# Computing the projection of a gated table in pieces between other products, with the results kept in DRAM

## The chip, the cores and the metric

One Trainium2 chip; the kernel runs on one of its cores. The metric is the device time of one execution in microseconds (us), median of the runs. All tensors are float32; a product of two float32 matrices is made of three matmuls of split operands (high x high, high x low, low x high), so every operand that enters TensorE is first split into a high part H (a cast on ScalarE) and a low part L = operand - H (a subtract on VectorE).

## The reference

One layer of a bidirectional hybrid encoder, 1024 positions, width 2048:

```python
z = rms_norm(h, norm_mix) @ w_in            # q, k, v, gate_a, u, gate_s
y_attn = block_attention(q, k, v) * silu(gate_a)
y_ssm = gelu(s5_bidirectional(u, ...))
glu = y_ssm @ w_glu + b_glu
y_ssm = glu[..., :1024] * sigmoid(glu[..., 1024:]) * silu(gate_s)
h = h + concatenate([y_attn, y_ssm]) @ w_out
gate = sigmoid(rms_norm(h, norm_ple) @ w_ple_gate)
h = h + gate * (p @ w_ple_proj)             # p: 1024 x 256
out = rms_norm(h, norm_final)
```

The change concerns the last product but one, `p @ w_ple_proj` (256 x 2048): it needs nothing that the layer computes, only inputs.

## The kernel before

Everything is transposed: a tile holds 128 features by positions. The work runs in stages whose instructions are written out by hand in one order for all engines (a manual schedule; each engine runs its own instructions in that order and waits on semaphores). In turn: the input projection with the state-space part beside it, attention (64 query blocks, `attention`, then four last iterations b = 64 to 67 that only finish blocks; 64 is NB), three stages of *units* in `back`, and the *gate*.

**Units.** Stages 0 (w_glu), 1 and 2 (halves of w_out) have 8 units each. A unit (`unit`) is a Strassen-like scheme of 7 products; a product is 4 x 3 = 12 matmuls of 512 columns into one PSUM tile `pr` (tag C, four buffers). Its weights are loaded by `sw_dma` (four 256 KB blocks a unit) and split by `sw_prep` three products ahead (two ScalarE copies, one VectorE subtract, L451, with a PSUM tile `hp` between). The result goes to the unit's thread (`u_glu`, `u_out`), which reads it on VectorE or ScalarE. All units of a stage share 28 split activation tiles `st` (4 per product). Those of the next stage are loaded (`put`) and split (`fill`, L311, in stage 2 L314) during the last unit, u = 7, into buffers that the products of that unit give back.

**Background work.** `bg` registers a generator; each `tick` advances all of them by one step and lets one waiting `fill` go out (four of five times in the units). There is a tick after each group of three matmuls of a unit's product and after every second group in the gate.

**Gate.** Two halves of 512 positions, in each 16 tiles n (`gate`): `mm_half` makes pg, 16 k-steps x 3 matmuls over w_gate, and then pp, 2 x 3 matmuls over w_proj, with the split halves of p that `p_load` makes at the start of each half. `fin_g` takes both: pg times the row scale, a sigmoid, times pp (L1352), plus h (on GpSimd, L1354). Weight blocks of 512 columns come through `w_dma` (three raw buffers) and `w_split`, in the order planned by `w_plan`, where each tile has four blocks of w_gate and one half-size block of w_proj. All DMAs are issued by SyncE's queue (SP), in program order.

## Time and profile before

| | |
|---|---|
| median of 3 runs | 2137.52 us (2135.57 to 2140.13) |
| profiled execution | 2138.92 us |
| its span, first to last instruction | 2137.1 us |
| mean granted TensorE clock | 0.989 of full speed |

A line such as L1185 is a line of the kernel before. PE is TensorE, PEld its weight loads, DVE VectorE, ACT ScalarE, POOL GpSimd, SP SyncE. In the windows PEclk is the clock granted to TensorE as a share of full speed, and "(x112)" a count of instructions. On a timeline a bracket gives the idle time of that engine before the instruction and what ended it. Matmuls are pipelined: the duration beside one is its latency, and the distance of two starts is what it costs.

### The profile page before, as it was taken

To read this page: it belongs to the slowest core of one execution; us is meant where nothing else is said; L and a number is where in the kernel's file an instruction comes from. 1 tells how busy PE (TensorE), PEld (TensorE's weight loads), DVE (VectorE), ACT (ScalarE), POOL (GpSimd) and SP (SyncE) were. 2 spreads that over 40 slices of the span, in tenths; PEclk is the share of its full clock that TensorE was granted. 3 is DMA by queue.
4 is the path that set the end of the run, shared out by engine and by line. 5 is a ranking of instruction groups with operands and counts; after the bars stand their busy time and mean duration, and the time that the engine had idled before them with its cause. 6 is when DMAs were issued, how large, how long until landed. Compare 5 with 4: busy or idle time off the path is not lost.

```text
span 2137.1 us, 29682 instructions
## 1 busy us (share of the span) xinstructions
PE 2064.0 (97%) x10140; PEld 1716.5 (80%) x10140; DVE 1475.1 (69%) x2406; ACT 901.2 (42%) x1615; POOL 922.8 (43%) x833
## 2 busy tenths in 40 slices
PE   8999999999999999998999999989999999999996
PEld 6888878888887877787889878878878778888885
DVE  7654787788877787847998976764677744465434
ACT  7111322122222222347777765654565633353332
POOL 0143455554655555513320556467565611221122
PEclk9999999999999999999999999999999999999998
DMA  6333223233333233454421366658765544455443
GB/s 217 91 107 104 78 72 113 83 84 95 94 85 109 79 88 94 143 173 148 158 70 50 129 236 213 227 194 285 252 200 168 173 143 125 134 183 168 148 117 123
DMA packets 183127, 296.51 MB, mean 139 GB/s; under 512 B 28352, under 2 KB 78656, under 8 KB 182720
## 3 DMA queue, kind: packets, MB, share of 16 engines
q1 hardware_dynamic: 181824, 292.51, 43.1%
q8 instruction: 81, 1.33, 0.3%
q10 hardware_dynamic: 1152, 2.10, 0.3%
q14 instruction: 70, 0.57, 0.1%
HBM read 211.37 MB, written 77.92 MB: 135 GB/s over the span
## 4 chain that ended last, share of the span: by engine, by line
PE 48%; DVE 8%; DMA 3%; ACT 2%; issue 2%; SPq 0%; POOL 0%; DVEq 0%; ACTq 0%
PE pr L1185 6%; PE pr L1186 6%; PE pr L1187 6%; PE pg L1325 5%; PE pg L1324 5%; PE pg L1326 5%; PE ptr L1017 2%; PE zgs L579 1%; PE zgs L580 1%; PE zgs L582 1%; PE S L987 1%; PE S L986 1%; PE S L990 1%; PE pv L1030 1%; PE pv L1031 1%
## 5 line engine op out<-in xcount | busy, mean ns | idle before, releaser
L311 DVE TENSOR_TENSOR wL<-wraw,wH 128x512 fp32r<-128x512 f32 x304 | 260.3, 870 | 317.0 <-ACT wH L310 312.9
L310 ACT CAST wH<-wraw 128x512 fp32r<-128x512 f32 x304 | 176.5, 595 | 302.2 <-PE zu L580 73.8
L1185 PE MATMUL pr<-st,wH 128*128 128x512 f32 x672 | 263.9, 393 | 11.9 <-DVE cx L1275 7.1
L1187 PE MATMUL pr<-st,wL 128*128 128x512 f32 x672 | 264.0, 393 | 0.4 <-DVE wL L451 0.4
L1186 PE MATMUL pr<-st,wH 128*128 128x512 f32 x672 | 263.6, 392 | 0.2 <-DVE st L311 0.2
L1326 PE MATMUL pg<-st,wL 128*128 128x512 f32 x512 | 200.1, 391 | 4.3 <-DVE wL L311 4.3
L1324 PE MATMUL pg<-st,wH 128*128 128x512 f32 x512 | 200.9, 392 | 0.7 <-ACT st L313 0.3
L1325 PE MATMUL pg<-st,wH 128*128 128x512 f32 x512 | 200.5, 392 | 0.6 <-DVE st L314 0.6
L1354 POOL TENSOR_TENSOR h<-cx,tz 128x512 f32<-128x512 f32 x31 | 40.8, 1318 | 295.0 <-DVE tz L1352 160.7
L1185 PEld LDWEIGHTS pr<-st,wH 128*128 128x128 f32 x672 | 127.3, 189 | 41.3 <-ACT st L310 5.9
L899 ACT COPY ks<-kp 16x224 f32<-16x224 f32 x32 | 10.8, 336 | 336.1 <-DVE ks L898 207.9
L1187 PEld LDWEIGHTS pr<-st,wL 128*128 128x128 f32 x672 | 127.3, 189 | 28.4 <-DVE wL L451 2.1
L1186 PEld LDWEIGHTS pr<-st,wH 128*128 128x128 f32 x672 | 127.2, 189 | 27.0 <-DVE st L311 0.6
L1326 PEld LDWEIGHTS pg<-st,wL 128*128 128x128 f32 x512 | 96.5, 189 | 25.3 <-DVE wL L311 5.1
L1324 PEld LDWEIGHTS pg<-st,wH 128*128 128x128 f32 x512 | 96.5, 188 | 23.1 <-ACT xsq L1342 1.0
L449 ACT CAST wH<-sraw 128x512 fp32r<-128x512 f32 x120 | 74.3, 619 | 96.7 <-PE pr L1186 75.9
L1267 POOL TENSOR_TENSOR cx<-cx,tz 128x512 f32<-128x512 f32 x64 | 87.8, 1384 | 62.6 <-DVE tz L1299 41.4
L1325 PEld LDWEIGHTS pg<-st,wH 128*128 128x128 f32 x512 | 96.4, 188 | 21.9 <-DVE st L314 1.3
L451 DVE TENSOR_TENSOR wL<-sraw,hp 128x512 fp32r<-128x512 f32 x120 | 81.9, 683 | 43.0 <-ACT hp L450 35.8
L772 POOL TENSOR_TENSOR tab<-pa 128x512 f32<-128x512 f32 x32 | 41.4, 1293 | 152.0 <-DVE r L907 152.0
L579 PE MATMUL zga<-hH,wH 128*128 128x512 f32 x256 | 104.6, 409 | 0.0
L579 PE MATMUL zq<-hH,wH 128*128 128x512 f32 x256 | 103.6, 405 | 0.0
(377 smaller groups left out, 5558.5 us busy)
## 6 DMA issues: line engine op xcount, KB each, us to landing
wraw<-in_w_in_dram SPq DMA_DIRECT2D x144, 256.0 KB
wraw<-in_w_gate_dram SPq DMA_DIRECT2D x128, 256.0 KB
sraw<-in_w_out_dram SPq DMA_DIRECT2D x64, 256.0 KB
st<-d_t SPq DMA_DIRECT2D x48, 256.0 KB
sraw<-in_w_glu_dram SPq DMA_DIRECT2D x32, 256.0 KB
cx<-in_xT_dram SPq DMA_DIRECT2D x16, 512.0 KB
d_p<-cx SPq DMA_DIRECT2D x16, 512.0 KB
cx<-d_p SPq DMA_DIRECT2D x16, 512.0 KB
```

The source lines that it names most:

```text
L310: nc.scalar.copy(H, src)
L311: nc.vector.tensor_tensor(L, src, H.bitcast(F32), ALU.subtract)
L449: self.nc.scalar.copy(H, raw)
L451: self.nc.vector.tensor_tensor(L, raw, hp, ALU.subtract)
L579: nc.tensor.matmul(ps[h], H[:, kk, :], rH[:, s], start=(k == 0), stop=False)
L1185: nc.tensor.matmul(ps, H[:, k], x[0], start=(k == 0), stop=False)
L1186: nc.tensor.matmul(ps, H[:, k], x[1], start=False, stop=False)
L1187: nc.tensor.matmul(ps, L[:, k], x[0], start=False, stop=(k == 3))
L1267: nc.gpsimd.tensor_tensor(x[:, h], x[:, h], u, ALU.add)
L1324: nc.tensor.matmul(ps, H[:, k % 4], x[0], start=(k == 0), stop=False)
L1325: nc.tensor.matmul(ps, H[:, k % 4], x[1], start=False, stop=False)
L1326: nc.tensor.matmul(ps, L[:, k % 4], x[0], start=False, stop=(k == nk - 1))
```

## The change

31 of the 32 projection products are made before or at the start of the gate, each as one *filler* (`filler`): 6 matmuls into a half of a PSUM tile `pp_ps`. Where they stand is listed in `F_AT` (stage, unit, product): four in the first unit of stage 0, four each in the last unit of stages 0, 1 and 2 and in the first of stages 1 and 2. Besides these there are four in the last four iterations of attention and three inside gate tile 0 (k = 1, 5, 9). The splits of p lie in the tiles "zz" and "t4" (`f_table`), made anew in unit 6 of each stage. Weights come in one raw tile `fR` and one split pair `fH`, `fL`; the results leave PSUM through one tile `po` and are stored in DRAM (`d_pp`). The gate loads them beside d_h into one tile (`x[:, 0]`, `x[:, 1]`); only its last tile still makes its product there. Further, the weight ring `sraw` has 5 buffers for 6, two small tiles `Bm` move to the pool of the state-space part, and the `hp` tiles take the halves of one PSUM tile for two tiles in turn.

```diff
@@ -249,2 +249,8 @@
 
+    F_AT = (
+        {(0, 0, i) for i in (1, 2, 4, 5)}
+        | {(s, 7, i) for s in range(3) for i in (3, 4, 5, 6)}
+        | {(s, 0, i) for s in range(1, 3) for i in (0, 1, 2, 4)}
+    )
+
     def __init__(self, ctx, tc, ins, out):
@@ -375,6 +381,7 @@
         self.w_end = len(q)
-        for _ in range(2):
+        for hf in range(2):
             for n in range(16):
                 tile_(self.i["w_gate"][n], 16)
-                tile_(self.i["w_proj"][n], 2)
+                if (hf, n) == (1, 15):
+                    tile_(self.i["w_proj"][n], 2)
         self.wq = q
@@ -427,3 +434,3 @@
             for j in blocks:
-                r = self.bk.tile([128, 512], F32, name="sraw", tag="sraw", bufs=6)
+                r = self.bk.tile([128, 512], F32, name="sraw", tag="sraw", bufs=5)
                 self.nc.sync.dma_start(r, self.su[u][j])
@@ -447,3 +454,3 @@
         raw = self.sr[src].rearrange("p (k m) -> p k m", m=128)
-        hp = self.ps.tile([128, 4, 128], F32, name="hp", tag="A", bufs=2)
+        hp = self.hp_ps[:, self.half(g % 2)].rearrange("p (k m) -> p k m", m=128)
         self.nc.scalar.copy(H, raw)
@@ -497,7 +504,2 @@
         self.rope_t = c.tile([128, 2, 64], F32, name="rope_t")
-        self.Bm = []
-        for j in range(2):
-            t = c.tile([128, 2, 2, 48], F32, name=f"Bm{j}")
-            nc.gpsimd.memset(t, 0.0)
-            self.Bm.append(t)
         self.rq = c.tile([128, NH * T], F32, name="rq")
@@ -525,2 +527,3 @@
         self.d_t = [[d(f"d_t{s}_{k}", (2, 128, SEQ)) for k in range(4)] for s in range(3)]
+        self.d_pp = [d(f"d_pp{n}") for n in range(KD)]
         self.d_pa = d("d_pa", (128, NG, NPA))
@@ -1173,3 +1176,3 @@
 
-    def unit(self, X, thread, nxt, hook):
+    def unit(self, s, u, X, thread, nxt, hook):
 
@@ -1192,2 +1195,4 @@
             hook(i)
+            if (s, u, i) in self.F_AT:
+                self.filler()
 
@@ -1313,2 +1318,63 @@
 
+
+    def f_table(self, hf):
+
+        self.fx = None
+        x = [self.t2k(tag, (128, 2, 512), F32R) for tag in ("zz", "t4")]
+        for k in range(2):
+            raw = self.bk.tile([128, 512], F32, name="po", tag="po", bufs=1)
+            self.nc.sync.dma_start(raw, self.i["pT"][k][:, self.half(hf)])
+            for _ in range(4):
+                yield
+            self.split(x[k][:, 0], x[k][:, 1], raw)
+            raw = None
+            yield
+        self.fx = x
+
+    def f_dma(self):
+        if self.fn < 31:
+            self.fraw = self.bk.tile([128, 256], F32, name="fR", tag="fR", bufs=1)
+            self.nc.sync.dma_start(self.fraw, self.i["w_proj"][self.fn % 16])
+            self.fn += 1
+
+    def f_split(self):
+        if self.fi < 31:
+            H, L = (self.bk.tile([128, 2, 128], F32R, name=t, tag=t, bufs=1) for t in ("fH", "fL"))
+            self.split(H, L, self.fraw.rearrange("p (k m) -> p k m", m=128))
+            self.fw, self.fraw = (H, L), None
+
+    def f_start(self):
+        self.f_dma()
+        for _ in range(5):
+            yield
+        self.f_split()
+        yield
+        self.f_dma()
+
+    def f_end(self, n, ps):
+        yield
+        o = self.bk.tile([128, 512], F32, name="po", tag="po", bufs=1)
+        self.nc.scalar.copy(o, ps)
+        self.f_split()
+        yield
+        self.f_dma()
+        yield
+        self.nc.sync.dma_start(self.d_pp[n % 16][:, self.half(n // 16)], o)
+
+    def filler(self):
+        n = self.fi
+        (H, L), self.fw = self.fw, None
+        ps = self.pp_ps[:, self.half(n % 2)]
+        for k in range(2):
+            x = self.fx[k]
+            self.nc.tensor.matmul(ps, H[:, k], x[:, 0], start=(k == 0), stop=False)
+            self.nc.tensor.matmul(ps, H[:, k], x[:, 1], start=False, stop=False)
+            self.nc.tensor.matmul(ps, L[:, k], x[:, 0], start=False, stop=(k == 1))
+            if k == 0:
+                self.tick()
+        self.fi += 1
+        del H, L
+        self.bg(self.f_end(n, ps))
+        self.tick()
+
     def mm_half(self, ps, nk, xs, each=None):
@@ -1411,3 +1477,3 @@
         for k in range(2):
-            H, L = (self.bk.tile([128, 512], F32R, name="sraw", tag="sraw", bufs=6) for _ in range(2))
+            H, L = (self.bk.tile([128, 512], F32R, name="sraw", tag="sraw", bufs=5) for _ in range(2))
             self.split(H, L, raw[k])
@@ -1424,4 +1490,5 @@
         hs, pT = [], {}
-        acc = self.t2k(("zz", "t4")[hf])
-        self.bg(self.p_load(hf, pT))
+        if hf == 1:
+            acc = self.t2k("t4")
+            self.bg(self.p_load(hf, pT))
         for n in range(16):
@@ -1430,4 +1497,7 @@
             pg = self.psC("pg")
-            ho = self.bk.tile([128, 512], F32, name="cx", tag="cx", bufs=4)
-            nc.sync.dma_start(ho, self.d_h[n][:, sl])
+            last = (hf, n) == (1, 15)
+            x = self.bk.tile([128, 2, 512], F32, name="cx", tag="cx", bufs=4)
+            nc.sync.dma_start(x[:, 0], self.d_h[n][:, sl])
+            if not last and (hf, n) != (0, 0):
+                nc.sync.dma_start(x[:, 1], self.d_pp[n][:, sl])
             if hf == 0 and n == 0:
@@ -1438,8 +1508,15 @@
                 self.mm_half(pg, 16, hg, lambda k: k < 15 and self.put_h(nhg, 1, [9 + k // 2], wait=3))
+            elif (hf, n) == (0, 0):
+                self.mm_half(pg, 16, hg, lambda k: self.fi < 31 and k % 4 == 1 and self.filler())
+                nc.sync.dma_start(x[:, 1], self.d_pp[n][:, sl])
+                self.fx = None
+                acc = self.t2k("zz")
             else:
                 self.mm_half(pg, 16, hg)
-            pp = self.psC("pp")
-            self.mm_half(pp, 2, pT)
+            pp = x[:, 1]
+            if last:
+                pp = self.psC("pp")
+                self.mm_half(pp, 2, pT)
             hs.append(hp[:, n % 2])
-            self.bg(self.fin_g(hf, n, pg, pp, ho, hs[n], acc))
+            self.bg(self.fin_g(hf, n, pg, pp, x[:, 0], hs[n], acc))
         if hf == 1:
@@ -1490,3 +1567,7 @@
                 self.bg(self.t_make(s + 1, stages[s + 1][0], self.four_sm, 14, 8))
-            self.unit(X, thread, units[n + 1][2] if n + 1 < len(units) else None, hook)
+            if u == 6:
+                self.bg(self.f_table(min(s, 1)))
+            elif u == 1:
+                self.fx = None
+            self.unit(s, u, X, thread, units[n + 1][2] if n + 1 < len(units) else None, hook)
             if u == 7:
@@ -1499,2 +1580,3 @@
         self.gate(0, hg, nhg)
+        assert self.fi == 31
         self.gate(1, nhg, None)
@@ -1569,2 +1651,7 @@
                 self.sp = ssm_pool.__enter__()
+                self.Bm = []
+                for n in range(2):
+                    t = self.sp.tile([128, 2, 2, 48], F32, name=f"Bm{n}", tag=f"Bm{n}")
+                    self.nc.gpsimd.memset(t, 0.0)
+                    self.Bm.append(t)
                 self.ssm_gen = self.ssm()
@@ -1583,2 +1670,10 @@
         for b in attn:
+            if b == NB - 5:
+                self.fn = self.fi = 0
+                self.bg(self.f_start())
+            elif b >= NB:
+                if b == NB:
+                    self.pp_ps = self.psA("pp_ps")
+                    self.hp_ps = self.psA("hp_ps")
+                self.filler()
             if b == 3:
@@ -1592,2 +1687,3 @@
                 self.sw_dma(0, range(4))
+                self.bg(self.f_table(0))
             elif b == NB - 4 or b == NB - 2:
```

## Rows read from the trace of the kernel before

**Rows 1.** The page, busy time of each engine, share of the span, instructions.
```profile
PE 2064.0 (97%) x10140; PEld 1716.5 (80%) x10140; DVE 1475.1 (69%) x2406; ACT 901.2 (42%) x1615; POOL 922.8 (43%) x833
```

**Rows 2.** TensorE's timeline inside a unit, first and last of 97 matmuls in sequence.
```profile
1359.73 0.39 PE L1187 MATMUL pr<-st,wL 128*128 128x512 f32 x1
...
1381.49 0.39 PE L1187 MATMUL pr<-st,wL 128*128 128x512 f32 x1
```

**Rows 3.** Instructions of line L1324 on tile pp: durations min/median/max in ns.
```profile
L1324 PE MATMUL pp<-sraw,wH x64: 392/394/398, 1725.7 to 2113.9; 128*128 128x512 f32 x64
```

**Rows 4.** Windows: busy us of PE, PEld, DVE, ACT, POOL, PEclk, DMA share, GB/s.
```profile
1226.00:1250.00 24.00, 22.25 (x97) 16.89 (x97) 20.18 (x28) 17.84 (x31) 9.02 (x7) 1.00 0.69 242
1380.00:1410.00 30.00, 23.61 (x88) 17.93 (x87) 29.38 (x37) 16.62 (x30) 16.43 (x13) 0.89 0.65 229
1395.00:1400.00 5.00, 5.00 (x16) 3.82 (x15) 4.89 (x8) 4.97 (x10) 3.08 (x3) 0.66 0.24 84
1535.00:1560.00 25.00, 20.68 (x84) 16.37 (x83) 25.00 (x29) 18.53 (x35) 19.30 (x14) 0.93 0.89 322
1704.00:1730.00 26.00, 19.52 (x76) 13.30 (x75) 15.54 (x33) 8.92 (x16) 6.73 (x5) 0.93 0.45 147
1730.00:2114.00 384.00, 383.23 (x1683) 314.83 (x1683) 180.77 (x260) 140.50 (x244) 78.43 (x60) 1.00 0.45 138
```

**Rows 5.** TensorE's timeline at the stage changes, the waits and two starts.
```profile
1217.69 1.06 PE L1017 MATMUL ptr<-ident,P 128*128 128x128 f32 x8 [1.19 <-ACT P L1002]
...
1221.70 1.06 PE L1017 MATMUL ptr<-ident,P 128*128 128x128 f32 x8 [1.51 <-DVE P L1010]
...
1388.41 0.47 PE L1185 MATMUL pr<-st,wH 128*128 128x512 f32 x1 [0.42 <-DVE tz L1251]
...
1394.64 0.47 PE L1185 MATMUL pr<-st,wH 128*128 128x512 f32 x1 [3.18 <-DVE tz L1253]
...
1404.85 0.47 PE L1185 MATMUL pr<-st,wH 128*128 128x512 f32 x1 [2.80 <-DVE cx L1275]
...
1555.47 0.47 PE L1185 MATMUL pr<-st,wH 128*128 128x512 f32 x1 [2.66 <-DVE cx L1275]
...
1709.18 0.50 PE L1326 MATMUL pg<-st,wL 128*128 128x512 f32 x1 [4.28 <-DVE wL L311]
...
1715.89 1.84 PE L345 MATMUL cs<-ones,xsq 128*128 128x1 f32 x16
...
1730.46 0.50 PE L1324 MATMUL pg<-st,wH 128*128 128x512 f32 x1 [0.15 <-ACT xsq L1342]
```

**Rows 6.** VectorE's timeline at the change from stage 0 to 1.
```profile
1387.59 0.68 DVE L1251 TENSOR_TENSOR tz<-pr,tz 128x512 f32<-128x512 f32 x1
...
1393.82 0.68 DVE L1253 TENSOR_TENSOR tz<-pr,tz 128x512 f32<-128x512 f32 x1
```

**Rows 7.** Instructions of single lines: durations min/median/max in ns, starts, forms.
```profile
L311 DVE TENSOR_TENSOR st<-st x64: 675/693/1826, 1221.5 to 1565.2; 128x512 fp32r<-128x512 f32 x64
...
L311 DVE TENSOR_TENSOR wL<-wraw,wH x304: 419/693/1784, 5.4 to 2108.8; 128x512 fp32r<-128x512 f32 x136, 128x256 fp32r<-128x256 f32 x16
...
L1275 DVE TENSOR_TENSOR cx<-pr,cx x64: 675/683/692, 1404.0 to 1710.3; 128x512 f32<-128x512 f32 x64
...
L1352 DVE TENSOR_TENSOR tz<-pp,tz x32: 691/692/694, 1733.5 to 2114.9; 128x512 f32<-128x512 f32 x32
...
L1215 ACT COPY tz<-pr x8: 567/574/589, 1232.4 to 1366.3; 128x512 f32<-128x512 f32 x8
```

**Rows 8.** The chain of waits, in order of time, two stage changes: start, us, what.
```profile
1368.31 5.99 DMA st<-d_t
...
1710.96 3.33 DMA d_h<-cx
```

**Rows 9.** ScalarE's timeline at the start of the gate.
```profile
1720.22 0.93 ACT L310 CAST wH<-wraw 128x512 fp32r<-128x512 f32 x2 [8.06 <-DMA wraw<-in_w_gate_dram]
```

**Rows 10.** SyncE's timeline at the start of the gate.
```profile
1715.25 0.38 SPq L387 DMA_DIRECT2D wraw<-in_w_gate_dram  x1
```

## Prediction, made before the change was run

> **What bounds the kernel now.** I read the page first, for the busy shares: TensorE is busy 97% of the span, the next, VectorE, 69% [rows 1]. So the time is TensorE's instructions plus the places where it stands still, and moving a product elsewhere can pay only if it falls into such a place. Next the timeline of TensorE inside a unit, for the price of one matmul: 96 start-to-start steps take 1381.49 - 1359.73 = 21.76 us, 0.2267 us each; the 0.39 us beside each row is latency, not cost [rows 2]. One projection product is 6 of these, 1.36 us; the 32 of them (three lines of 64) take 43.5 us in the gate stage [rows 3].
>
> Third, the windows, for where TensorE is idle [rows 4]. In the gate stage, 1730 to 2114, it is idle 0.8 of 384 us: there every matmul removed is time removed. Idle time and half clock stand at the four stage changes. I take idle as window minus busy, and the clock as (1 - PEclk) of the window:
> - (a) attention to units of stage 0: 1.75 us in 1226:1250, plus two waits of 1.19 and 1.51 us in the tail of attention [rows 4, 5]: 4.45 us.
> - (b) stage 0 to 1, 1380:1410: 6.39 idle + 0.11 x 30 = 3.3 clock: 9.7 us.
> - (c) stage 1 to 2, 1535:1560: 4.32 + 1.75: 6.1 us.
> - (d) stage 2 to gate, 1704:1730: 6.48 + 1.8: 8.3 us.
>
> Together 28.5 us: the most that filling can bring. The single waits show the shape of it: 3.18 and 2.80 us in (b), 2.66 in (c), 4.28 in (d), each followed by a stretch at the lower clock level (1395:1400 at 0.66) [rows 4, 5]. All wait for VectorE. Its timeline shows why: at 1388.41 TensorE wants the PSUM buffer of the product three before, which ended near 1387.84 - 3 x 2.72 = 1379.7 and was read only at 1387.59; the next was read at 1393.82, 11 us after its matmuls [rows 5, 6]. VectorE is busy 29.4 of the 30 us from 1380 on [rows 4], splitting the 28 tiles of the next stage beside its evictions. So in (b) and (c) TensorE does not lack work by accident: VectorE is behind.
>
> **The change, part by part.** *Removed and added on TensorE.* 31 products leave the gate: 31 x 1.36 = 42.2 us off a stage without idle time. The same 42.2 us come back as fillers: 8 at (a) (four in the attention tail, four in the first unit), 8 at (b), 8 at (c), 7 at (d) (four in the last unit, three inside gate tile 0). The sum is zero; the gain is what idle time they fill, less what the new work makes late.
>
> *New work of the others.* Each filler brings a split of 128x256 (a cast on ScalarE, a subtract on VectorE from 0.42 us), a PSUM copy by ScalarE (0.57), a 128 KB load, a 256 KB store and later a 256 KB load [rows 7]. The w_proj splits leave the gate, where VectorE had 384 - 181 = some 200 us to spare anyway [rows 4], and land where it has none. Subtracts with both inputs in SBUF (L311 on st) take 0.68 to 1.83 us for 512 columns, while instructions with one input in PSUM (L1275, L1352) stay at 0.68 to 0.69 [rows 7]. So the filler's subtract, half as wide, costs 0.42 to 0.9 us; I take 0.5, as the median of L311 is near its minimum. The gate's multiply (L1352) gets an SBUF operand in place of one in PSUM: at the worst of L311 it is 1.1 us slower, 31 x 1.1 = 35 us in a stage where VectorE has 200 to spare, so nothing at the end. The Trainium skill (SBUF — State Buffer, section "SBUF: two separate sides") says that VectorE and GpSimd take a shared port pair exclusively, so that a VectorE instruction with two SBUF inputs blocks behind a GpSimd one that reads SBUF. The trace agrees with it by the 0.68 and 1.83 us above; it speaks against the change, and its price is in the 0.42 to 0.9.
>
> *The coupling, which decides the sum.* A product's weights are split three products ahead, and its PSUM may wait three more; that is how TensorE could run 8 to 11 us ahead of VectorE. A filler's weights are split only after the filler before it, in one buffer, two ticks after it is issued: some nine matmuls, 2 us of TensorE's time, before the next filler. So where VectorE is over 2 us behind, the next filler itself waits, and the matmuls queued behind it.
>
> (b): the unit across 1404.85 ends 24 matmuls and one clock dip later, 1404.85 + 5.44 + 1.6 = 1411.9 [rows 5]. After the change its last filler needs a split that VectorE reaches between 1404 + 7 x 0.5 = 1407.5 and, if the whole busy stretch to 1410 comes first, 1410 + 8 x 0.5 = 1414 [rows 4]. Then 1.36 + 5.44 us: 1414.3 to 1420.8, that is 2.4 to 8.9 later for 10.9 us of work taken from the gate. Gain 2.0 to 8.5; I take 5, near the middle, since both bounds come from the same stretch.
>
> (c): VectorE's lag is smaller (waits of 2.66 and under [rows 5]); with 10.9 us of filler TensorE's own queue is longer than the lag. Gain up to 6.1; less 1 for late splits, 5; low bound 2.
>
> (a): the tail's iterations are a chain through ScalarE and VectorE, and the first half's table adds two more splits (0.69 us each on VectorE [rows 7]) to it. Of 4.45 I leave 1 idle and pay 1: 2.5; bounds -1 and 4.45.
>
> (d): the four fillers before the gate cover the 4.28 us wait [rows 5]. The next wait is new. Gate tile 0's fourth weight block is loaded only when SyncE is past the stores of d_h (3.33 us) and the loads that wait for them, from 1715.25 on, and ScalarE sits 8.06 us until 1720.22 for it [rows 8 to 10]. The split of the second gate filler stands behind this cast on ScalarE. TensorE, starting the gate near 1704.3 + 5.4 = 1709.7, reaches that filler after 24 matmuls and the 1.8 us column sum [rows 5], at 1717. The cast comes near 1722 (four filler splits, 2 us, make VectorE's closing L1275 and the stores later), its own split near 1723: 6 us of wait and 1.7 of clock. With 42 matmuls and the row broadcast tile 0 ends near 1736, now 1730.46 [rows 5]: 5.6 late for 6 x 1.36 = 8.2 us of work (seven fillers less its own projection). Gain 2.6, say 3; up to 8.3 if the load comes early; 0 below.
>
> *Costed at nothing:* the gate's extra load (256 KB per 12 us, DMA share 0.45 [rows 4]); the smaller weight ring (5 buffers, five alive at most; the block that now waits is needed five products later); the moved Bm tiles (two small memsets); PSUM of tag A, still two halves for hp and two for the filler. If a d_pp load came late, the multiply would hold up VectorE's weight splits, three blocks (8 us) ahead of TensorE.
>
> Sum: 2.5 + 5 + 5 + 3 = 15.5 us. The profiled execution took 2138.92, 1.8 more than its span; it becomes 2123.4. It stands 1.4 above the median, so 2122 for the median.
>
> **The rivals.**
> 1. *All idle time is filled:* 28.5 less 2.5 us: 2111.5. For it: TensorE's added 9.5 to 10.9 us at each change exceed the waits. Against: the coupling, and ScalarE's wait in (d).
> 2. *The fillers lock TensorE to VectorE, and the wait moves into the fillers:* low bounds of all four, -1 + 2.1 + 2 + 0 = 3 us: 2134.5, or nothing at all. For it: the 11 us lag [rows 6]. Against: four fillers of 1.36 us give VectorE time as well.
> 3. *Slower: the one staging buffer.* Projection weights apart, each result is copied by ScalarE into one buffer, and the next copy waits until the store has landed, with every H cast behind it. Fillers follow each other every 18 matmuls, 4.08 us. The copy takes 0.57 [rows 7]; for the landing I have 3.33 us (a 512 KB store) and 5.99 us (a 256 KB load at a busy time) [rows 8]. So 0.57 + 3.33 - 4.08 < 0, or 2.5 us of stall for some 23 intervals, 57 us on ScalarE. If 0.7 of that reaches TensorE, 40 - 28.5: 2149. It decides from 28.5 / 23 = 1.24 us an interval, a landing of 4.75 us. The Trainium skill (DMA: Bandwidth & Descriptors, "Anatomy of one DMA — SWDGE (gpsimd) path") fits 2.0 us plus bytes over 436 GB/s, an estimate of 2.6 us for 256 KB, on another issue path; by it this rival falls. No run here shows it for this store.
>
> **How the numbers follow.** Forecast 0.52 (range of its own 2116 to 2129), rival 1 0.20, rival 2 0.18, rival 3 0.10. About 0.2%, 4.3 us, is what a measurement here can tell from no change: the border is 2133.2. The forecast and rival 1 are faster, rival 2 half so: 0.81. Same: the other half of rival 2 and a little of 3: 0.10. Slower: 0.09. The range reaches from rival 1 nearly through rival 2: 2110 to 2135.
>
> **What would show it.** Gate stage from its second tile on: 42.2 us fewer, less tile 0's share, with no new idle time. In (b) waits of TensorE for fH or fL (the filler's weights) of 1 to 4 us, one clock dip or none. In (d) the 4.28 us wait gone, and one near 6 us in gate tile 0 for a filler's weights. ScalarE waiting for the landing of d_pp over 1 us a time would speak for rival 3. The prediction is wrong if those filler waits are missing (then rival 1) or if the four changes lengthen by the whole 42 us (then rival 2).

## The result and the profile after

The changed kernel takes 2164.28 us (median), the kernel before 2138.34 on the same chip: ratio 1.0118, 95% interval 1.0097 to 1.0138. It is 25.9 us slower. The forecast was 2122; its range, 2110 to 2135, does not hold the time, and the sign is wrong. The execution profiled took 2165.69 us.

First the page of after, the busy times:

```profile
PE 2076.0 (96%) x10140; PEld 1726.7 (80%) x10140; DVE 1467.4 (68%) x2412; ACT 919.9 (43%) x1652; POOL 915.9 (42%) x833
```

The number of matmuls is that of [rows 1], as the change says. TensorE's busy time rose by 12.0 us for the same matmuls, while its mean granted clock fell from 0.989 to 0.982; its idle time (span 2163.9 less busy) rose by 14.8 us. The other engines' busy times moved by less than 20 us each. So the shares don't show where the time went. The windows (columns as in [rows 4]) around the four changes of stage, and the gate:

```profile
1226.00:1250.00 24.00, 21.16 (x102) 17.70 (x101) 15.08 (x22) 15.48 (x30) 6.19 (x5) 0.82 0.44 146
1380.00:1425.00 45.00, 38.76 (x160) 30.40 (x158) 38.20 (x51) 29.21 (x55) 22.60 (x17) 0.96 0.80 275
1550.00:1595.00 45.00, 37.14 (x157) 30.17 (x156) 30.91 (x43) 26.75 (x49) 26.33 (x21) 0.90 0.81 286
1718.00:1760.00 42.00, 39.90 (x175) 32.41 (x174) 31.92 (x44) 30.20 (x52) 26.36 (x20) 1.00 0.65 218
1775.00:2140.00 365.00, 359.35 (x1579) 295.77 (x1578) 170.44 (x252) 136.31 (x230) 79.17 (x61) 0.99 0.52 167
```

TensorE still stands idle 2.8, 6.2 and 7.9 us in the first three windows, with a clock down to 0.82, although it was given more products to do at each of these places. The waits of TensorE (us in total, times, longest) from 1180 to 1830 say for what:

```profile
PE pp_ps L1370 <- ACT fH L316: 25.8, 9, 7.9
PE pp_ps L1372 <- DVE fL L317: 8.5, 7, 2.5
```

The waits of [rows 5] for tz, cx and wL, 0.42 + 3.18 + 2.80 + 2.66 + 4.28 = 13.3 us, are gone; in their place stand 34.3 us, all before matmuls of fillers and none before those of a unit. (4.4 us more stand before transposes of the attention tail.) And ScalarE, in the same stretch:

```profile
ACT po L1357 <- DMA d_pp<-po: 34.7, 19, 7.7
```

Its copy of a result into `po` waits 19 times for the store of the result before to land. One such place in full, on the timelines of TensorE, ScalarE, VectorE and SyncE:

```profile
1578.88 0.39 PE L1370 MATMUL pp_ps<-zz,fH 128*128 128x512 f32 x1
...
1590.99 0.79 PE L1370 MATMUL pp_ps<-zz,fH 128*128 128x512 f32 x1 [7.86 <-ACT fH L316]
...
1576.76 0.58 ACT L1357 COPY po<-pp_ps 128x512 f32<-128x512 f32 x1
...
1590.05 0.58 ACT L1357 COPY po<-pp_ps 128x512 f32<-128x512 f32 x1 [7.70 <-DMA d_pp<-po]
1590.53 0.41 ACT L316 CAST fH<-fR 128x256 fp32r<-128x256 f32 x1
...
1578.07 0.93 DVE L317 TENSOR_TENSOR fL<-fR,fH 128x256 fp32r<-128x256 f32 x1
...
1577.38 2.89 SPq L1268 DMA_DIRECT2D cx<-d_p  x2
1580.37 2.02 SPq L1103 DMA_DIRECT2D st<-d_t  x4
1582.78 0.33 SPq L1337 DMA_DIRECT2D fR<-in_w_proj_dram  x1
1583.37 0.32 SPq L1362 DMA_DIRECT2D d_pp<-po  x1
```

Read it along the data. A result is copied at 1576.76. Its store goes out only at 1583.37, because SyncE's queue first issues six loads of the next stage and then the filler's next weight load. (The subtract that frees that load's buffer had ended at 1579.00, so here the loads ahead held the queue.) When the store lands, the next copy starts, at 1590.05. Behind that copy, on ScalarE, is the cast of the next filler's weights (1590.53), and behind that the filler (1590.99) and every matmul after it. The chain of waits (start, us, what) has these six landings:

```profile
1240.02 2.30 DMA d_pp<-po
...
1249.76 6.18 DMA d_pp<-po
...
1414.94 2.62 DMA d_pp<-po
...
1421.60 4.42 DMA d_pp<-po
...
1583.37 6.60 DMA d_pp<-po
1607.73 4.03 DMA d_pp<-po
```

Over all 19 copies that waited, a store took 2.34 to 6.68 us from its issue to the start of the copy that it released, and ScalarE's copies started 4.09 to 13.62 us apart.

For the comparisons below I cut the execution by starts of matmuls on TensorE's timeline: *tail*, from the 51st block's pv matmuls in attention to the first unit; *u0*, unit (0, 0); *b*, from unit (0, 7) to (1, 1); *c*, from (1, 7) to (2, 1); *d*, from (2, 7) to gate tile 1; *gate*, from there to the last pg. The last column is the change of the five stretches against before. The stretches take in 31 fillers (four each in tail and u0, eight each in b and c, seven in d) and give up gate tile 0's own product: 30 x 1.36 = 40.8 us of matmuls, so +40.8 means that no idle time was filled. Each row is one execution, which can lie off its median (that of "one copy only" by 5.3 us, that of after by 1.4).

```
                 ratio   tail    u0     b      c      d     gate   sum   against before
before             -     46.57  22.02  48.68  44.74  45.21  382.54 207.2    -
after            1.0118  61.08  30.41  60.92  62.66  58.66  339.24 273.7  +66.5
no store         1.0049  57.13  28.30  59.68  58.33  56.22  339.16 259.7  +52.4
one weight pair  1.0038  58.95  28.96  59.76  58.78  51.75  339.30 258.2  +51.0
one copy only    0.9976  54.47  25.72  58.16  52.67  51.27  339.11 242.3  +35.1
matmuls only     0.9908  53.71  24.56  49.07  49.07  53.04  339.32 229.5  +22.2
```

The gate gives back 43.3 us. The stretches grow by 66.5: all of the moved 40.8, and 25.7 more. The sums of the five windows, before and after, divide these:

```profile
sum 207.22, PE 184.75 PEld 149.24 DVE 177.68 ACT 137.45 POOL 106.70; mean PE 36.95 PEld 29.85 DVE 35.54 ACT 27.49 POOL 21.34
sum 273.73, PE 234.80 PEld 188.81 DVE 196.68 ACT 170.82 POOL 116.96; mean PE 46.96 PEld 37.76 DVE 39.34 ACT 34.16 POOL 23.39
```

TensorE's idle time in them goes from 22.5 to 38.9 us, 16.5 more; its busy time rises by 50.05, which is 9.2 more than the moved matmuls, at granted clocks of 0.91 to 0.97 after where before has 0.93 to 1.00. Together with the gate that is 23.2 of the 25.9 us between the medians; the rest lies ahead of the stretches, in a part that lasts 1174.5 to 1183.9 us in the executions kept here.

### The profile page after: what moved, and what is told of

It is laid out like the page before. It is cut to its first block, busy times and chain, and to the rows that moved or that the text cites. A ratio compares the mean times of both kernels' runs of the same rounds, so it can differ in the third digit from the quotient of the medians.

```text
span 2163.9 us, 29834 instructions
## 1 busy us (share of the span) xinstructions
PE 2076.0 (96%) x10140; PEld 1726.7 (80%) x10140; DVE 1467.4 (68%) x2412; ACT 919.9 (43%) x1652; POOL 915.9 (42%) x833
## 4 chain that ended last, share of the span: by engine, by line
PE 53%; DVE 9%; DMA 4%; ACT 2%; issue 1%; SPq 1%; POOL 0%; DVEq 0%; ACTq 0%
PE pr L1188 6%; PE pr L1189 6%; PE pr L1190 6%; PE pg L1390 5%; PE pg L1392 5%; PE pg L1391 5%; PE ptr L1020 2%; PE zgs L582 2%; PE zgs L583 2%; PE zgs L585 2%; DMA d_pp<-po 1%; DVE mx L1000 1%; DVE PTL L1024 1%; PE S L990 1%; PE S L989 1%
## 5 line engine op out<-in xcount | busy, mean ns | idle before, releaser
L317 DVE TENSOR_TENSOR wL<-wraw,wH 128x512 fp32r<-128x512 f32 x273 | 242.8, 905 | 298.4 <-ACT wH L316 298.1
L316 ACT CAST wH<-wraw 128x512 fp32r<-128x512 f32 x273 | 164.2, 616 | 278.1 <-PE zu L583 78.9
L1420 POOL TENSOR_TENSOR h<-cx,tz 128x512 f32<-128x512 f32 x31 | 40.4, 1303 | 258.9 <-DVE tz L1418 196.9
L458 DVE TENSOR_TENSOR wL<-sraw,hp_ps 128x512 fp32r<-128x512 f32 x120 | 82.2, 685 | 50.9 <-ACT hp_ps L457 43.5
L582 PE MATMUL zgs<-hH,wH 128*128 128x512 f32 x256 | 103.1, 403 | 0.0
```

What stands on the lines that cost most here:

```text
L316: nc.scalar.copy(H, src)
L317: nc.vector.tensor_tensor(L, src, H.bitcast(F32), ALU.subtract)
L458: self.nc.vector.tensor_tensor(L, raw, hp, ALU.subtract)
L582: nc.tensor.matmul(ps[h], H[:, kk, :], rH[:, s], start=(k == 0), stop=False)
```

## Experiments

Ratios are to the kernel before, measured on the same chip, with 95% intervals.

**1. No store.** The store at the end of `f_end` is left out; the gate loads d_h[n] in place of d_pp[n].

```diff
-        yield
-        self.nc.sync.dma_start(self.d_pp[n % 16][:, self.half(n // 16)], o)
...
```

> Left out: the store of each filler's result; the gate multiplies by a second copy of d_h, loaded in place of d_pp. So traffic to DRAM falls by 31 x 256 KB and nothing waits for a landing. Theory L (the one staging buffer: ScalarE waits 34.7 us in 19 places for stores to land, the next filler's weight cast stands behind that wait, and TensorE waits 25.8 us for fH): these two waits nearly vanish and the time falls from 2164 to about 2138 (2128 to 2145). Rival V (VectorE's lag holds the fillers, the store only makes it visible): TensorE's waits for fH and fL stay above 20 us in sum and the time stays at 2152 to 2164.

2147.75 us, 1.0049 [1.0033, 1.0065]: 0.69% better than after, about 15 us, but still slower than before. ScalarE no longer waits for a landing; TensorE still waits for the weights:

```profile
PE pp_ps L1368 <- ACT fH L316: 18.1, 7, 5.3
PE pp_ps L1370 <- DVE fL L317: 8.9, 9, 2.4
```

The time lies between the two ranges that were expected. So the store, its landing and its traffic together, is a cause of over half the loss, and not the only one.

**2. The split ahead of the copy.** In `f_end` the split of the next weights comes before the copy that waits for the landing.

```diff
+        self.f_split()
         o = self.bk.tile([128, 512], F32, name="po", tag="po", bufs=1)
         self.nc.scalar.copy(o, ps)
-        self.f_split()
```

> Only the order on ScalarE changes: the next filler's weights are split before the result is copied out, so the cast of fH no longer stands behind the wait for a landing; the waits of the copy stay. Theory L in the form that the weight cast carries the wait to TensorE: TensorE's 25.8 us of waits for fH fall below 8 and the time to 2140 to 2150. If the wait reaches TensorE by another way (casts of wH and st behind the copy): waits move there, and the time stays at 2155 to 2164. Rival V: no change, 2160 to 2166.

2154.95 us, 1.0081 [1.006, 1.0103], 0.37% better than the change. The waits for the weights' cast become waits for the copy, at about the same length:

```profile
PE pp_ps L1370 <- ACT po L1358: 27.5, 10, 6.9
PE pp_ps L1372 <- DVE fL L317: 7.6, 5, 2.4
```

**3. The store right behind the copy**, ahead of the next weight load on SyncE's queue.

```diff
         self.nc.scalar.copy(o, ps)
+        self.nc.sync.dma_start(self.d_pp[n % 16][:, self.half(n // 16)], o)
         self.f_split()
         yield
         self.f_dma()
-        yield
-        self.nc.sync.dma_start(self.d_pp[n % 16][:, self.half(n // 16)], o)
```

> Only the order on SyncE changes: the store goes out right after the copy, ahead of the load of the next projection weights, which waits for VectorE's split. The trace shows copy end 1227.5 and store issue 1228.99, up to 6 us apart at a busy place (1577.3 to 1583.4). Theory L: the landing comes 1.5 us earlier or more, ScalarE's 34.7 us of waits for d_pp fall to about 15 and the time to 2148 to 2156. Rival V: within 4 us of 2164.

2154.45 us, 1.0075 [1.0059, 1.009]. ScalarE's waits for the landing fall from 34.7 to 9.7 us, TensorE's for the cast from 25.8 to 21.9. A third of the loss was the store's place in the queue, as theory L expected.

**4. Two staging halves.** The first 20 results are staged in the two halves of `xsq`, which nothing uses in stages 0 and 1.

```diff
-        o = self.bk.tile([128, 512], F32, name="po", tag="po", bufs=1)
+        if n < 20:
+            o = self.xsq[:, self.half(n % 2)]
+        else:
+            o = self.bk.tile([128, 512], F32, name="po", tag="po", bufs=1)
```

> Two staging buffers in place of one for the first 20 fillers (the halves of xsq, unused in those stages), the one of before for the last 11. Theory L: at the changes attention to stage 0 and stage 0 to 1, and in the last unit of stage 1, waits of ScalarE for d_pp vanish; of the 21 us that these two changes and the half of the third cost beyond their fillers' matmuls, 10 to 16 come back: 2148 to 2154. Rival V: within 4 us of 2164.

2155.55 us, 1.0076 [1.0056, 1.0096]. ScalarE's waits for landings before those 20 copies vanish (9.8 us are left, before the last 11); TensorE still waits 25.4 us for the cast. The time is 1.5 us above the range expected from theory L.

**5. One weight pair.** All fillers use the first weights; no loads and splits between them. The stores stay.

```diff
...
-        self.f_split()
-        yield
-        self.f_dma()
...
-        (H, L), self.fw = self.fw, None
+        H, L = self.fw
```

> Left out: the loads and splits of the projection weights after the first; all fillers use the first weights. Stores and copies stay. Theory W (the one weight pair: a filler waits for a split issued only after the filler before it, 25.8 us for fH and 8.5 for fL in the changed kernel, still 18.1 and 8.9 without stores): these waits vanish, and the time falls from 2164 to 2128 to 2145, the upper end if ScalarE's waits for the landings (34.7 us) now reach TensorE through the casts of wH and st. Rival V (VectorE's lag of old): waits of TensorE for VectorE's evictions come back in their place, and the time stays above 2150.

2147.09 us, 1.0038 [1.0019, 1.0057]. This lies between the two ranges that were expected. Without weights to wait for, the fillers wait 25.3 us for the copy instead. (With the weight load gone the store also goes out one tick earlier than in the change.)

**6. One copy only.** Experiments 1 and 5 together: six matmuls and a copy out of PSUM are left of a filler.

> Left out: the loads and splits of the projection weights after the first, and the stores of the results (the gate loads d_h twice). What stays of a filler is six matmuls and one copy. It shows what the places themselves give. If the idle time of before can be filled there: 2108 to 2125, with next to no waits at the changes. If VectorE's own lag is what TensorE waits for (rival V): 2125 to 2140, with waits for cx, tz and st as before the change.

2132.68 us, 0.9976 [0.9963, 0.9989]. The first version that is faster than before, and by little. The time falls in the rival's range, but the waits are neither for cx nor for tz nor for st: they are for the copy. TensorE's waits, and then one place on the timelines of TensorE, ScalarE and VectorE:

```profile
PE pp_ps L1363 <- ACT po L1355: 15.6, 9, 4.4
```

```profile
1386.85 0.39 PE L1363 MATMUL pp_ps<-zz,fH 128*128 128x512 f32 x1
...
1395.54 0.80 PE L1363 MATMUL pp_ps<-zz,fH 128*128 128x512 f32 x1 [4.43 <-ACT po L1355]
...
1384.45 0.58 ACT L1355 COPY po<-pp_ps 128x512 f32<-128x512 f32 x1
1393.12 0.72 ACT L1237 ACTIVATE tq<-tq,vec 128x512 f32<-128x512 f32 x1 [6.02 <-DVE tq L1232]
...
1394.91 0.58 ACT L1355 COPY po<-pp_ps 128x512 f32<-128x512 f32 x1
...
1392.41 0.68 DVE L1232 TENSOR_TENSOR tq<-pr,tz 128x512 f32<-128x512 f32 x1
```

The filler of 1386.85 is copied only at 1394.91, since ScalarE stands 6.02 us before an instruction of a unit's thread, L1237, whose input VectorE makes late. The next filler writes the other half of `pp_ps`, which was free from 1385.0 on (1384.45 + 0.58), and yet starts when the copy at 1394.91 ends.

**7. Two of everything.** Two `po`, two pairs fH, fL, the split first and the store right behind the copy (one activation buffer less, 32 for 33, to make room).

```diff
-    NBIG = 33
+    NBIG = 32
...
-            H, L = (self.bk.tile([128, 2, 128], F32R, name=t, tag=t, bufs=1) for t in ("fH", "fL"))
+            H, L = (self.bk.tile([128, 2, 128], F32R, name=t, tag=t, bufs=2) for t in ("fH", "fL"))
...
-        o = self.bk.tile([128, 512], F32, name="po", tag="po", bufs=1)
+        self.f_split()
+        o = self.bk.tile([128, 512], F32, name="po", tag="po", bufs=2)
         self.nc.scalar.copy(o, ps)
+        self.nc.sync.dma_start(self.d_pp[n % 16][:, self.half(n // 16)], o)
```

> Nothing left out: two weight pairs and two staging buffers in place of one, the split ahead of the copy and the store right behind it; the 4 KB for it come from the ring of big tiles (32 for 33). Theories L and W together: waits of TensorE for fH and fL under 8 us, of ScalarE for d_pp under 5; time 2118 to 2138. If the smaller ring of big tiles costs as much as the buffers bring: 2145 to 2160. Rival V: no better than without the stores, 2147.

2153.84 us, 1.0071 [1.0052, 1.009]. No wait for a landing is left, and none for weights; the fillers wait for the copy instead, more than in experiment 2:

```profile
PE pp_ps L1372 <- ACT po L1361: 30.7, 11, 6.3
```

The time falls in the range that was expected if the smaller ring of activation buffers costs as much as the buffers bring. Experiment 13 has the same ring, without fillers, and is not slower than before.

**8. Away from the changes.** Fillers 16 to 30 inside units 1 to 5 of stage 2, after products 1, 3 and 5; none at the changes (c) and (d).

```diff
-        | {(s, 7, i) for s in range(3) for i in (3, 4, 5, 6)}
-        | {(s, 0, i) for s in range(1, 3) for i in (0, 1, 2, 4)}
+        | {(0, 7, i) for i in (3, 4, 5, 6)}
+        | {(1, 0, i) for i in (0, 1, 2, 4)}
+        | {(2, u, i) for u in range(1, 6) for i in (1, 3, 5)}
...
```

> Nothing left out: the last 15 fillers stand in the inner units 1 to 5 of stage 2 (after products 1, 3 and 5), none at the changes stage 1 to 2 and stage 2 to gate. The first 16 stay. Inside a unit there is no idle time to fill and little backlog. If a filler there costs its six matmuls alone: the two changes go back to 44.7 and 44 us (from 62.7 and 58.7), the inner units grow by 20.4; 2164 - 32.4 + 20.4 = 2152 (2148 to 2156). If a filler brings waits wherever it stands: 2158 to 2168.

2147.47 us, 1.0039 [1.0025, 1.0054], 0.79% better than the change and better than the 2148 to 2156 expected. Stretch c is back at 45.29 (44.74 before). The units inside the stages grow from 342.90 to 363.32 us: 20.4 = 15 x 1.36, the bare matmuls. So the same filler, with copy, split, load and store, costs nothing beside its matmuls where the other engines have slack. What it costs at a change is that place's. Stretch d, with no filler and without tile 0's own product and the splits of p ahead of it, takes 38.62 us here, 6.6 less than before, and the gate 342.40, 3.2 more than in the change. So the seven fillers at (d) cost the change 20.0 - 3.2 = 16.8 us for 9.5 us of matmuls, more than the comparison with before shows.

**9. Matmuls only.** Experiment 6 without the copy.

```diff
-        o = self.bk.tile([128, 512], F32, name="po", tag="po", bufs=1)
-        self.nc.scalar.copy(o, ps)
```

> Leaves out: the copy of the projection results out of PSUM, their store, and all projection weights but the first (the gate multiplies by h in place of them). What is left of a filler is six matmuls that no other engine follows. Theory (the fillers are held by ScalarE's copy): TensorE's waits before filler matmuls, 15.6 us in the kernel with one copy, fall under 2 us; the five stretches around the changes, together 242.3 us there and 207.2 before for 40.8 us of matmul work, fall by 8 to 14 us, and the time comes 8 to 14 us below that kernel, near 2121. Rival (VectorE's backlog sets the length whatever the fillers do): the waits move to the products' matmuls, the stretches stay above 239 us and the time within 3 us of 2132.7.

2116.65 us, 0.9908 [0.9892, 0.9925], below the 2121 that was expected. No filler waits at all. The windows of [rows 4], (b) and (c), in this kernel:

```profile
1380.00:1410.00 30.00, 30.00 (x133) 24.78 (x132) 27.41 (x36) 19.51 (x36) 18.90 (x14) 1.00 0.68 245
1535.00:1560.00 25.00, 25.00 (x112) 20.66 (x111) 23.00 (x29) 18.65 (x33) 17.14 (x13) 1.00 0.94 327
```

TensorE is busy throughout at full clock. By the table, b holds its 10.9 us of fillers within 0.4 us of its old length and c within 4.3. Both are 49.07 us long; their 216 matmuls at 0.2267 make 48.97, so nothing is left to fill in either. The tail with u0 and d fill next to nothing (9.7 and 7.8 us longer, for 10.9 and 8.2 of matmuls). In d the wait is still there, one step later, on TensorE and ScalarE:

```profile
1739.94 3.78 PE L364 MATMUL bc<-tq,ones 128*128 128x512 f32 x4 [4.18 <-DVE tq L358]
...
1733.47 0.62 ACT L316 CAST wH<-wraw 128x512 fp32r<-128x512 f32 x1 [7.27 <-DMA wraw<-in_w_gate_dram]
...
1737.65 0.21 ACT L338 ACTIVATE tq<-tq 128x8 f32<-128x8 f32 x1
```

ScalarE waits for a gate weight block as in [rows 9], and the square root for the row scale (L338) is behind it on its queue.

**10 and 11. Halves or tiles.** Both start from experiment 6 and split the units' weights without the PSUM tile `hp`; that frees one tile of tag A. The first keeps `pp_ps` as one tile of two halves, the second gives the fillers two tiles in turn.

```diff
-        ps = self.pp_ps[:, self.half(n % 2)]
+        ps = self.pp_ps[n % 2][:, self.half(0)]
...
-                    self.pp_ps = self.psA("pp_ps")
+                    self.pp_ps = [self.psA("pp_ps") for _ in range(2)]
```

> The kernel with nothing but six matmuls and one copy a filler (no store, first weights throughout; the gate multiplies by h in place of the results), and the units' weights are split without their PSUM copy hp: VectorE subtracts from SBUF alone. It is the control for the next kernel. Theory (ScalarE's queue paces the fillers): one ScalarE copy less a product, and no wait of it for VectorE's subtract, so 0 to 6 us faster than 2132.7 if the subtracts stay near 0.69 us; if the subtract with two SBUF inputs grows to over 1 us, VectorE is later and the time is equal or up to 10 us longer.

> As the kernel without hp (same parts left out), but the fillers use two PSUM tiles in turn where they used two halves of one. Theory (the two halves count as one buffer, so a filler waits for the copy of the one directly before it): TensorE's waits for that copy fall to less than half, the time falls by 4 to 10 us against the kernel without hp. Rival (the halves are independent already and the waits come from something else): same waits, time within 2 us of it.

With one tile 2136.63 us, 0.9994 [0.9979, 1.0009]; with two 2131.39, 0.9977 [0.9967, 0.9986]. Waits of TensorE, of the first and of the second:

```profile
PE pp_ps L1361 <- ACT po L1353: 20.3, 9, 4.4
```

```profile
PE pp_ps L1361 <- ACT po L1353: 4.0, 2, 3.6
PE bc L364 <- DVE tq L358: 4.3, 1, 4.3
PE pr L1186 <- DVE cx L1278: 3.9, 1, 3.9
PE pg L1381 <- ACT wH L316: 3.2, 1, 3.2
```

The waits for the copy fall to a fifth: in this kernel the two halves of a tile do count as one buffer. Of the 16.3 us only 5.2 come back in the medians, whose intervals overlap. Other waits are there in their place, for bc, cx and a gate weight, 11.4 us; and the executions profiled are the fastest of the first kernel (2129.60) and the slowest of the second (2135.76), so what the second tile is worth in time stays open. The first, expected 0 to 6 us below experiment 6, came out 4 us above it: without `hp` the subtract of the units' weights reads two inputs from SBUF and takes 980 ns on average (120 on sraw), where experiment 6 has 669 to 690.

**12. Copies made late.** Four products only: fillers after products 5 and 6 of the last unit of stages 0 and 1, with weights split ahead of them and copies 30 ticks behind them, inside the next stage. The other 28 stay in the gate. There are 32 activation buffers, as in experiment 7.

```diff
-    F_AT = (
...
+    F_AT = {(0, 7, 5): 2, (0, 7, 6): 3, (1, 7, 5): 4, (1, 7, 6): 5}
...
     def f_end(self, n, ps):
-        yield
+        for _ in range(30):
+            yield
```

> The whole layer is computed. Only four projection products are moved: two into the last unit of stage 0 and two into that of stage 1 (after products 5 and 6). Both weight pairs and the table of p are split during unit 6 and the start of unit 7, ahead of the fillers; the results stay in the two halves of their PSUM tile and are copied and stored 30 ticks later, inside the next stage. The other 28 products stay in the gate. Theory (a filler is free where no copy, split or store is tied to it at the change, as the six matmuls alone showed with 10.5 and 6.6 us filled at the two changes): the gate is 5.4 us shorter, the two changes grow by no more than 1 us each, the time is 3 to 5.5 us below before, near 2133. Rival (the added splits at the change from VectorE's full stretch cost what the fillers fill): the changes grow by 2.7 us each or more, the time is within 2 us of before or above it.

**13. No filler.** Experiment 12 with an empty list: the smaller weight ring, Bm in the other pool and hp in halves of one tile are what is left of the change, with 32 activation buffers.

> The whole layer is computed, all 32 projection products in the gate as before. Left of the change are only the parts that the prediction costed at nothing: five buffers in the weight ring for six, Bm in the other pool, hp in the halves of one PSUM tile (and one big activation buffer less, 32 for 33, as in the kernel with two buffers of everything). Theory (they cost nothing): within 2 us of before. Rival (the halves of one PSUM tile tie ScalarE's hp copy to VectorE's subtract of the product before): the changes grow by 1 to 4 us each and the time by 3 to 10 us.

2135.15 us, 0.9986 [0.9975, 0.9997], and 2134.82, 0.9986 [0.9974, 0.9998]. The parts costed at nothing cost nothing; the median of 13 is 3.5 us below before, where 2 had been expected at most. In experiment 12, b is 48.72 us long (before 48.68) with 2.7 us more work, c 47.00 (44.74; 1 us more had been expected at most), and the gate 376.35 (382.54): by these stretches some 4 us are gained. The medians of 12 and 13 don't show it. Whether four late fillers pay stays open; at best they bring 0.2%.

## Why the prediction was wrong

**The step that failed is "The coupling, which decides the sum".** It let a filler wait for one thing, the split of its own weights, and let VectorE be 2 us late before that hurt; from this it took gains of 2.5, 5, 5 and 3 us. Measured against their matmuls, the four places lost: tail and u0 12.0 us (22.9 longer for 10.9), b 1.3, c 7.0, d 5.3. A filler is tied to the other engines by three cycles, each one filler long: copy to next filler, since the halves of `pp_ps` are one buffer; copy to store to next copy, by `po`; split to filler to next split, by fH and fL. All three run through ScalarE's queue, which the unit's own instructions hold for up to 6.02 us when VectorE is late (experiment 6). The Trainium skill (PSUM — Partial Sum Buffer, section "Engine vs sequencer instructions") says that the queues of ScalarE, VectorE and GpSimd are strictly first in, first out; the rows of experiment 6 agree: the copy at 1394.91 stands behind the instruction that waited 6.02 us. I had counted the copy as 0.57 us of work and never as something that the next filler waits for; the landing stood in rival 3 alone. Of the 25.7 us that the five stretches lost, 16.5 are idle time and 9.2 lower clock; the sum allowed for one dip of the clock at (b), 1.6 us, and one at (d), 1.7.

**What each tie costs**, from the ratios, in us of 2138: the matmuls alone -19.7 (0.9908); the copy +14.5 (0.9976 less 0.9908); the store +13.3 (1.0038 less 0.9976); the weights +15.6 (1.0049 less 0.9976); store and weights together 1.5 more (to 1.0118). Sum +25.2. Each figure is the difference of two ratios and carries 4 to 5 us of their intervals, so the last cannot be told from nothing. Each takes in the work and the traffic as well as the wait, and the store is priced at experiment 5's earlier place. These are costs in the absence of the others. Freed singly, a tie hands much of its wait to the next: experiments 2, 4 and 7 remove the waits that they aim at and get back 8 to 10 us, not more. By the table the ties differ from place to place (one execution each, differences in us): at (b) the copy is 9.1 of the 11.9 between the bare matmuls and the change; at (c) the copy is 3.6, the weights 5.7, the store 6.1.

**What bounds the kernel** was read rightly: the idle time at (b) and (c) is open to matmuls that nothing follows (experiment 9: 10.9 - 0.4 = 10.5 us filled where I had counted 9.7, and 10.9 - 4.3 = 6.6 for 6.1). So was the gate: 43.3 us shorter where the 30 products removed behind tile 0 make 40.8 by 1.36 each. From tile to tile it takes 12.30 us before and 10.88 after (first pg matmuls at 1742.89 and 1755.19, at 1796.75 and 1807.63), so a product cost 1.42 there; that makes 42.6.

**(a)** was forecast at +2.5. Even the bare matmuls fill only 1.2 us there, and the whole change loses 12.0, the most of all places, with the clock at 0.82 from 1226 to 1250. Between the bare matmuls (9.7 us longer than before) and the change (22.9), the table has the copy at 1.9 us, the weights at 5.2 and the store at 7.7; what the table's splits take of the 9.7 was not measured apart.

**(d)** was forecast at +3 with a wait near 6 us for a filler's weights in gate tile 0. That wait came, and from the late weight block on ScalarE as foreseen:

```profile
1785.61 0.79 PE L1370 MATMUL pp_ps<-zz,fH 128*128 128x512 f32 x1 [5.53 <-ACT fH L316]
...
1783.54 0.62 ACT L316 CAST wH<-wraw 128x512 fp32r<-128x512 f32 x1 [7.82 <-DMA wraw<-in_w_gate_dram]
```

So did the two waits of 1 to 4 us for fH at (b): 2.30 us at 1413.05 and 1.89 at 1427.04. The signs of the one lock that I saw came true; the price did not. That the late block (7.27 us in experiment 9) would still hold back the row scale, so that filling before it gains nothing (0.4 us against before; against experiment 8, which has no filler there, 14.4 - 3.1 = 11.3 us longer for 9.5 of matmuls), was not seen.

**The rivals.** Rival 1 comes true where the ties are cut, at (b) and (c); with (a) and (d) unfilled that is 2116.65 for 2111.5. Rival 2, the lock, has the mechanism, but its price stopped at no gain: I took it that a locked filler can at worst leave the idle time as it was. It added to it in every version with a copy and one more tie; that the unit's matmuls behind a waiting filler make VectorE's next input late in turn would explain it, but is argued, not measured. The sign that was to speak for it came: the changes lengthened by more than the whole 42 us. Rival 3, the staging buffer, is real too: it alone had the right sign, its 2149 is the nearest of all to 2164, and the store is over half of the loss (experiment 1). ScalarE's waits for landings, 1.8 us on average, are the sign that it named. Of the 19 landings only two (6.26 and 6.68 us) pass the 4.75 us from which it was to decide, but its sum let the store go out with the end of the copy: in the trace the store is issued 0.61 to 7.36 us after the copy starts, and so the next copy comes 4.09 to 13.62 us after the one before, in all 19 places over the 4.08 between fillers. I gave it 0.10, partly because the page's figure argued against it. The Trainium skill (DMA: Bandwidth & Descriptors, "Anatomy of one DMA — SWDGE (gpsimd) path") gives the fit by which I estimated 2.6 us, for another issue path; ten of the 19 landings, 2.34 to 2.70 us, agree with it, and the two longest, at DMA shares of 1.00 and 1.02, do not: there the measurement decides.

**The costs at nothing** held: experiment 13, and the gate's multiply, which with both inputs in SBUF takes 692 ns on average, as with one in PSUM [rows 7]. The filler's subtract, taken at 0.5 us within 0.42 to 0.9, took 677 ns on average and up to 1528:

```profile
L1418 DVE TENSOR_TENSOR tz<-cx,tz 128x512 f32<-128x512 f32 x31 | 21.5, 692 | 21.6 <-ACT tz L1414 21.6
L317 DVE TENSOR_TENSOR fL<-fR,fH 128x256 fp32r<-128x256 f32 x31 | 21.0, 677 | 29.1 <-ACT fH L316 26.1 <-PE pr L1190 2.6
...
L317 DVE TENSOR_TENSOR fL<-fR,fH x31: 410/426/1528, 1216.0 to 1790.9; 128x256 fp32r<-128x256 f32 x31
```

On the timelines of VectorE and GpSimd the two differ in this: of the 31 subtracts 14 overlap an instruction of GpSimd and take 987 ns on average; the other 17 take 421. None of the gate's multiplies overlaps one: GpSimd's next instruction, L1420, waits for the multiply's result.

## What to carry to other kernels

In this kernel, work moved into the idle time of the bounding engine paid in full only where no other engine had to follow it there (-0.92%); one copy per piece left a quarter of that (-0.24%), and everything that the piece needs turned it into a loss. So list for each moved piece every buffer that it takes and gives back, and ask how many pieces may be in flight before the first buffer comes back through a late queue. One piece in flight, by whichever buffer, is a lock, and freeing one of several such buffers moved most of the wait to the next. An experiment that leaves all followers out and adds them back one at a time prices such a lock sooner than one that doubles the buffers one by one.

## What the runs showed of the hardware that was not expected

The same 256 KB store landed in 2.30 us at 1240 (DMA share 0.52 meanwhile) and in 6.60 at 1583 (share 1.03), among the loads of the next stage: a factor of 2.9 within one execution. Below that the share does not order the landings: 4.33 us at 0.30, 2.47 at 0.74.

A VectorE subtract with both inputs in SBUF depended on GpSimd's instructions beside it: in experiment 10 the 133 of 168 unit subtracts that overlap one take 1085 ns on average, the other 35 take 682; in experiment 6, with one input in PSUM, 120 of 168 overlap one and all take 669 to 690.

In experiment 9, eight products more at (b) and at (c) did not only fill the waits but kept the granted clock at 1.00, where [rows 4] had 0.89 and 0.93.
